# Gate and up of four feed-forward blocks: column tiles in pairs, as seven block products instead of eight

## The chip, the core and the metric

The kernel runs on one core of a Trainium2 chip. The metric is the device time of one execution in microseconds (us). TensorE (PE) multiplies, VectorE (DVE), ScalarE (ACT) and GpSimd (POOL) work on elements, SyncE (SP) issues the transfers.

## What is computed

Two pairs of transformer layers on 512 tokens of width 1024. Each of the four layers ends in a gated feed-forward block, and these four blocks are what the change touches:

```
def swiglu(xn, w_gate, w_up, w_down):
    return (jax.nn.silu(xn @ w_gate) * (xn @ w_up)) @ w_down
```

The hidden width is 2816 = 22 x 128 in all four. Around them stand a mixer of retention, dilated attention and gated MLP (twice), a sparse attention with pooling, a convolution module and two cross attentions, which the change leaves alone.

## The kernel before

All matrix products are made from fp32 numbers split in two fp32r parts, high and low: `mm3` issues three matmuls (high x high, high x low, low x high) for each block of 128 x 128 weights. The activations stand transposed in `xh` and `xl` (8 blocks of 128 features, 512 tokens). The weights come from one stream, `ws`, in the order of use, in tiles of 128 x 1024: `_Weights.prefetch` issues a transfer on SP's queue into one of three `raw` buffers, `_Weights.pump` has ScalarE cast a tile to its high part and VectorE subtract to get the low part, into one of eight `hl` slots. `get` hands out the next tile, `done` gives a slot back.

`ffn` is the block. A column tile of gate or of up (`prod(n, j, ...)`, n the tile, j = 0 gate, 1 up) is 8 blocks x 3 matmuls with the weights stationary and tokens moving, into one PSUM bank. The head of the block makes the tiles n = 0, 1 for tokens 0 to 255, then finishes the norm and the transposes of the last 128-token rows that the stage before left pending (`pend`), then the same tiles for tokens 256 to 511. After that the other 20 tiles of gate and of up run over all 512 tokens. `evac` applies silu on ScalarE into `sg` and multiplies with up on VectorE into `hraw`. The down projection follows, with 22 steps of 24 matmuls; `hsplit` splits a tile of `hraw` in two parts for it.

The order of instructions is written out: a list of `steps` is run by `_Clock`, each step with a length in us that is only used to decide when a transfer counts as arrived and when pending pieces of the norm are due. Each engine runs its instructions in the order in which they are issued, and waits on semaphores.

Of the kernel before, what the change touches and what calls it, by code (L numbers as in the profile page):

```python
# [19 lines left out]
P = 128  # L20
T = 512
# [53 lines left out]
def _weight_tiles(a):  # L75
# [8 lines left out]
    def pairs(w0, w1):  # L84
        for n in range(w0.shape[1] // P):
            yield _rows(w0[:, n * P:(n + 1) * P], 0, KD)
            yield _rows(w1[:, n * P:(n + 1) * P], 0, KD)

    for l in range(DEPTH):
        for name, n in CHUNKS_1:  # L90
            yield from moving(a["w_in"][l][:, COLS_1[name]:COLS_1[name] + n])
        w = a["w_out"][l]
        yield from by_rows(np.concatenate([w[384:768], w[768:1024], w[0:384]]))
        yield from pairs(a["w_gate_up"][l][:, :NF * P], a["w_gate_up"][l][:, NF * P:])
        yield from by_rows(a["w_down"][l])
    for l in range(DEPTH):
# [22 lines left out]
        yield from by_rows(a["cross_wo_2"][l])  # L119
        yield from pairs(a["ffn_w_gate_2"][l], a["ffn_w_up_2"][l])  # L120
        yield from by_rows(a["ffn_w_down_2"][l])
# [70 lines left out]
class _Weights:  # L192
    def __init__(self, nc, raw, hl, src, widths, depth, slots, clock):
# [8 lines left out]
        self.limit = slots  # L202
        self.splits = 0

    def prefetch(self, upto=1 << 30):
        while self.loaded < min(len(self.widths), self.split + self.depth, upto):
            j = self.loaded
            w = abs(self.widths[j])
            self.r[j] = self.raw.tile([P, D], F32, tag="raw", name="raw")
# [4 lines left out]
            self.loaded += 1  # L214

    def pump(self, most=BURST, force=False):
        while most:
# [3 lines left out]
            if self.split < self.loaded and self.splits < self.released + min(self.limit, self.slots):  # L221
# [4 lines left out]
                r = self.r.pop(j)  # L226
                t = self.hl.tile([P, 2, D], F32R, tag="hl", name="hl")
# [4 lines left out]
                self.splits += 1  # L232
                moved = True
            if not moved:
                return

    def get(self):
        j = self.taken
        self.taken += 1
        while j not in self.t and self.widths[j] > 0:  # L240
            self.pump(1, True)
        w = self.widths[j]
        if w < 0:
            self.split += 1
            return self.r.pop(j)[:, :-w], None
        t = self.t.pop(j)
        return t[:, 0, :w], t[:, 1, :w]

    def done(self):
        self.released += 1  # L250


@with_exitstack
def tile_mixers(ctx: ExitStack, tc: tile.TileContext, a: dict, widths: list, out: bass.AP):
# [41 lines left out]
    X = _Clock()  # L296
    W = _Weights(nc, _Bufs(3), _Bufs(8), a["ws"], widths, 3, 8, X)

    def load_x(t):
# [5 lines left out]
    def blocks(b, n=128):  # L305
        return b.rearrange("p (a c) -> p a c", c=n)
# [104 lines left out]
    def g1(key, ts, n, banks, held, evac, fetch=True, free=True, src=None, pump=None):  # L411
# [3 lines left out]
        def step(i):  # L415
            def go():
                if i == 0:
                    st["b"] = [bank(j) for j in banks]
                if fetch:
                    held[key, i] = W.get()  # L420
                wh, wl = (None if w is None else blocks(w, n) for w in held[key, i])
                for kk in range(2):
                    k = 2 * i + kk
                    for b, t in zip(st["b"], ts):
                        if wl is None:
                            PE.matmul(b[:, :n], src[0][:, k, cols(t)], wh[:, kk], start=k == 0, stop=k == KD - 1)
                            continue
                        mm3(b[:, :n], sh[:, k, cols(t)], sl[:, k, cols(t)], wh[:, kk], wl[:, kk], k == 0, k == KD - 1)
                if free:
                    held.pop((key, i))  # L430
                    if wl is not None:
                        W.done()
                if pump is not None:
# [59 lines left out]
    def ffn(pend, post, nxt, last=False):  # L493
# [8 lines left out]
        def evac(n, c0, c1):  # L502
            sg = pl.tile([P, T], F32, tag="sg", name="sg", bufs=2)
            gb, ub = st[n]
            S.activation(sg[:, c0:c1], gb[:, c0:c1], AF.Silu)  # L505
            V.tensor_mul(hraw[:, n, c0:c1], sg[:, c0:c1], ub[:, c0:c1])  # L506

# [24 lines left out]
        steps += [(0.9, p) for p in pend]  # L532
        for n in range(2):
# [7 lines left out]
        hsp = {}  # L541

        def hsplit(k):
            if k < NF:
                hh = pl.tile([P, T], F32R, tag="hh", name="hh", bufs=5)
                hl = pl.tile([P, T], F32R, tag="hlw", name="hlw", bufs=5)
                split_from(hh, hl, hraw[:, k, :])
                hsp[k] = (hh, hl)

# [31 lines left out]

        for i in range(2):
            j = len(steps) - 3 + i
            steps[j] = (steps[j][0], lambda f=steps[j][1], i=i: (f(), hsplit(i)))
        for k in range(NF - TAIL):
# [1166 lines left out]
```

## Time and profile before

| what | value |
|---|---|
| median of 3 runs | 2831.24 us (2827.76 to 2839.96) |
| the profiled execution | 2833.05 us, span of its instructions 2831.3 us |
| mean granted TensorE clock | 0.988 |
| busy share: TensorE, VectorE, ScalarE, GpSimd | 97%, 45%, 36%, 18% |
| transfers | 256 MB, 90 GB/s over the span |

The busy share of an engine is an average over stages with different limits. A matmul's record overlaps the next one's, so a matmul's cost in a stream is the step from start to start.

### The profile page before, as it was taken

Reading aid. Unit: us, or ns where it says so; the run is one execution under the profiler, and the core shown is the slowest. Engines: PE = TensorE matmul, PEld = TensorE weight load, DVE = VectorE, ACT = ScalarE, POOL = GpSimd, SP = SyncE. Lnnn points to the kernel's source line nnn. Section 1 sums busy time; section 2 is a strip of 40 time slices with the busy share of each in tenths; the row PEclk is TensorE's granted clock in tenths of the full one; section 3 lists DMA queues with packets and bytes.
Section 4 is the critical chain, followed back from the end, with each engine's and each line's share of the span. In section 5 each row is a group of like instructions: output and inputs, shape, how many; then the busy total and the mean of one; then the engine's idle time right before and its main releaser. Section 6 shows DMA issues by size and latency. Waiting matters only on the chain.

```text
span 2831.3 us, 34304 instructions
## 1 busy us (share of the span) xinstructions
PE 2739.1 (97%) x13688; PEld 2300.4 (81%) x13688; DVE 1275.2 (45%) x1940; ACT 1018.8 (36%) x1783; POOL 496.7 (18%) x495
## 2 busy tenths in 40 slices
PE   8999999999999999999999999999998889999999
PEld 7888888889788888888677888888886678888887
DVE  4565222344464232454875433233379654432232
ACT  4434222333433222234454433223257445322231
POOL 3231000003131000022461310000049813000000
PEclk9999999999999999999999999999999999999999
DMA  4222322323122223323132213223232212123231
GB/s 156 74 73 75 114 95 97 112 62 109 58 82 85 92 93 108 112 66 107 53 123 82 91 37 119 89 99 124 90 118 90 97 38 90 53 93 101 94 114 52
DMA packets 76192, 255.96 MB, mean 90 GB/s; under 512 B 10368, under 2 KB 11776, under 8 KB 76032
## 3 DMA queue, kind: packets, MB, share of 16 engines
q1 hardware_dynamic: 76032, 253.77, 27.4%
q8 instruction: 107, 1.75, 0.3%
q14 instruction: 53, 0.43, 0.0%
HBM read 251.64 MB, written 2.10 MB: 90 GB/s over the span
## 4 chain that ended last, share of the span: by engine, by line
PE 84%; DVE 8%; ACT 3%; issue 2%; POOL 2%; DMA 0%; ACTq 0%; POOLq 0%; SPq 0%; DVEq 0%
PE b L315 26%; PE b L317 26%; PE b L316 26%; DVE hl L229 1%; DVE b L1527 1%; PE b L337 1%; PE b L1407 1%; PE b L1560 1%; ACT hl L228 1%; DVE mask L1185 1%; PE b L716 1%; POOL sm L322 1%; DVE xn L354 0%; DVE mask L1190 0%; PE b L751 0%
## 5 line engine op out<-in xcount | busy, mean ns | idle before, releaser
L315 PE MATMUL b<-xh,hl 128*128 128x512 f32 (+1 forms) x1728 | 641.2, 371 | 1.6 <-ACT xh L325 1.6
L316 PE MATMUL b<-xl,hl 128*128 128x512 f32 (+1 forms) x1728 | 640.5, 371 | 1.7 <-DVE xl L326 1.7
L317 PE MATMUL b<-xh,hl 128*128 128x512 f32 (+1 forms) x1728 | 639.9, 370 | 0.0
L229 DVE TENSOR_TENSOR hl<-raw,hl 128x1024 fp32r<-128x1024 f32 (+1 forms) x408 | 482.9, 1208 | 152.2 <-ACT hl L228 149.0
L228 ACT CAST hl<-raw 128x1024 fp32r<-128x1024 f32 (+1 forms) x468 | 465.1, 1015 | 114.6 <-PE b L317 76.6
L315 PE MATMUL b<-hl,xh 128*128 128x512 f32 (+2 forms) x1152 | 440.2, 382 | 3.0 <-ACT xh L1630 1.6
L316 PE MATMUL b<-hl,xh 128*128 128x512 f32 (+2 forms) x1152 | 423.6, 368 | 2.0 <-DVE hl L229 2.0
L317 PE MATMUL b<-hl,xl 128*128 128x512 f32 (+2 forms) x1152 | 424.2, 368 | 0.3
L315 PEld LDWEIGHTS b<-xh,hl 128*128 128x128 f32 x1728 | 326.6, 189 | 58.5 <-ACT xh L325 2.8
L316 PEld LDWEIGHTS b<-xl,hl 128*128 128x128 f32 x1728 | 326.5, 189 | 57.6 <-DVE xl L326 2.7
L317 PEld LDWEIGHTS b<-xh,hl 128*128 128x128 f32 x1728 | 326.5, 189 | 55.3
L506 DVE TENSOR_TENSOR hraw<-sg,b 128x512 f32<-128x512 f32 (+1 forms) x96 | 61.8, 643 | 675.3 <-PE b L317 669.7
L505 ACT ACTIVATE sg<-b 128x512 f32<-128x512 f32 (+1 forms) x96 | 54.0, 562 | 673.2 <-PE b L317 673.1
L315 PE MATMUL b<-hl,hh 128*128 128x512 f32 x704 | 274.4, 390 | 0.0
L317 PE MATMUL b<-hl,hlw 128*128 128x512 f32 x704 | 273.9, 389 | 0.0
L316 PE MATMUL b<-hl,hh 128*128 128x512 f32 x704 | 273.9, 389 | 0.0
L315 PEld LDWEIGHTS b<-hl,xh 128*128 128x128 f32 x1152 | 220.1, 191 | 33.2 <-issue 7.0
L316 PEld LDWEIGHTS b<-hl,xh 128*128 128x128 f32 x1152 | 220.2, 191 | 26.1 <-DVE hl L229 3.4
L317 PEld LDWEIGHTS b<-hl,xl 128*128 128x128 f32 x1152 | 219.2, 190 | 26.7 <-DVE xl L326 1.5
L229 POOL TENSOR_TENSOR hl<-raw,hl 128x1024 fp32r<-128x1024 f32 (+2 forms) x60 | 142.3, 2388 | 81.7 <-ACT hl L228 81.5
L326 DVE TENSOR_TENSOR hlw<-hraw,hh 128x512 fp32r<-128x512 f32 x88 | 60.3, 689 | 210.2 <-ACT hh L325 210.2
L317 PEld LDWEIGHTS b<-hl,hlw 128*128 128x128 f32 x704 | 132.2, 188 | 27.4
(272 smaller groups left out, 2974.7 us busy)
## 6 DMA issues: line engine op xcount, KB each, us to landing
raw<-in_ws SPq DMA_DIRECT2D x400, 512.0 KB, 3.5
raw<-in_ws SPq DMA_DIRECT2D x64, 384.0 KB, 3.1
x<-in_x SPq DMA_DIRECT2D x4, 512.0 KB, 6.4
mem<-in_mem SPq DMA_DIRECT2D x4, 512.0 KB, 5.9
out<-x SPq DMA_DIRECT2D x4, 512.0 KB, 2.6
raw<-in_ws SPq DMA_DIRECT2D x4, 336.0 KB, 2.8
gain<-in_g_mix_pre SPq DMA_DIRECT2D x2, 512.0 KB, 5.6
gain<-in_g_mix_post SPq DMA_DIRECT2D x2, 512.0 KB, 4.3
```

What stands on the lines that cost most here:

```text
L228: self.nc.scalar.copy(t[:, 0, :w], r[:, :w])
L229: self.low.tensor_sub(t[:, 1, :w], r[:, :w], t[:, 0, :w].bitcast(F32))
L315: PE.matmul(o, lh, rh, start=first, stop=False)
L316: PE.matmul(o, lh, rl, start=False, stop=False)
L317: PE.matmul(o, ll, rh, start=False, stop=last)
L322: G.tensor_tensor(dst, dst, nhalf[:, :n], op=OP.pow)
L326: (low or V).tensor_sub(dl, src, dh.bitcast(F32))
L337: PE.transpose(b[:, kk * P:(kk + 1) * P], xn[:, k * P:(k + 1) * P], ident)
L505: S.activation(sg[:, c0:c1], gb[:, c0:c1], AF.Silu)
L506: V.tensor_mul(hraw[:, n, c0:c1], sg[:, c0:c1], ub[:, c0:c1])
L716: PE.matmul(s[hh][:, :n], qkT["aq"][rs, pr, cols(t)], qkT["ak"][rs, pr, :n], start=True, stop=True)
L1185: V.scalar_tensor_tensor(mask[t], w[:, :n], iw[:, t, h:h + 1], acc, op0=OP.mult, op1=OP.add)
```

## The change

The tiles n = 0, 1 and the head stay. The other 20 tiles of gate and 20 of up are taken two by two: a unit is a pair of column tiles (n, n + 1) of gate or of up, 256 columns x 1024 features of weights, over 512 tokens. The activations are cut in four blocks (features 0 to 511 or 512 to 1023, tokens 0 to 255 or 256 to 511) and the weights in four (features, column tile), and the unit's result is made of seven products of such blocks or of sums of them, each 4 blocks x 3 matmuls of 256 tokens, into banks 0 to 4 and half of bank 5 or 6 each (`todo` in `seven`). Two units, gate and up, make a pair of hidden tiles; there are 20 units in each block.

The sums of activations are made once for each block in the head, full sums in unused parts of `hraw` (`whole`, `mix`), then high and low parts (`sum_high`, `sum_low`) in new `sh` tiles or in `xh`, `xl`. The sums of weights are made for each unit (`_Weights.unit`): `t13` two differences of 512 columns on GpSimd, `t24` two on VectorE, in place in the raw tiles, then four slots are cast and subtracted (`cast1`, `low1` to `cast3`, `low3`; slot 4 has 512 columns). The preparation of unit i + 1 is issued between the products of unit i. The sums of results are a copy on ScalarE (`m1`) and six VectorE instructions in `s2`, `s4`, `s5`, `s6` and `whole_sum`. silu runs in place on a pair of tiles, and `gated` multiplies a pair. The second raw tile of a unit goes to the two `xn` buffers. The gains of the next stage (`nxt`) are loaded after gate and up instead of in the head.

```diff
+    def seven(w0, w1):
+        yield from pairs(w0[:, :2 * P], w1[:, :2 * P])
+        for n in range(2, w0.shape[1] // P, 2):
+            for w in (w0, w1):
+                for c in (n, n + 1):
+                    yield _rows(w[:, c * P:(c + 1) * P], 0, KD), True
...
+        def t13():
+            b = u["b"] = self.r.pop(u["j"])
+            u["b12"], u["b22"] = (b[:, 512 * i:512 * i + 512] for i in range(2))
+            G.tensor_sub(u["b11"], u["b12"], u["b11"])
+            G.tensor_sub(u["b12"], u["b12"], u["b22"])
+
+        def t24():
+            V.tensor_sub(u["b22"], u["b22"], u["b11"])
+            V.tensor_sub(u["b21"], u["b21"], u["b22"])
...
-        for n in range(2, NF):
-            for j in range(2):
-                steps.append(prod(n, j, 0, 512, True, True))
-        steps[8] = (steps[8][0], lambda f=steps[8][1]: (nxt(), f()))
...
+        def product(i, x, w, o):
+            (xa, xb), (wa, wb) = act[x], unit(i)["w" + w]()
+            for k in range(4):
+                mm3(o, wa[:, k], wb[:, k], xa[:, k], xb[:, k], k == 0, k == 3)
...
+            def whole_sum():
+                V.tensor_add(c[:, :, 256:], u3[:, None, :].to_broadcast([P, 2, 256]), halves(b45))
+                if not j:
+                    S.activation(c, c, AF.Silu)
+
+            def gated():
+                if j:
+                    V.tensor_mul(hraw[:, n:n + 2, :], hraw[:, n:n + 2, :], c)
+            done.append((whole_sum, gated))
+            last = done[-2] if i else (lambda: None,) * 2
+
+            def s0():
+                last[0]()
+                W.done(int(i > 0))
+                prep(i + 1, "low1")
+
+            def s1():
+                S.copy(m1, p1)
+                prep(i + 1, "t13")
+                last[1]()
+
+            def s2():
+                V.tensor_add(c[:, 0, TOK[0]], m1, p2)
+                prep(i + 1, "cast4")
+                W.done()
+
+            def s3():
+                prep(i + 1, "low4")
+                W.done()
+
+            def s4():
+                V.tensor_add(u2, m1, p6)
+                prep(i + 1, "t24", "cast2")
+
+            def s5():
+                V.tensor_add(u3, u2, p7)
+                prep(i + 1, "low2", "cast3")
+                W.done()
+
+            def s6():
+                V.tensor_add(u4, u2, p5)
+                V.tensor_add(c[:, 1, TOK[0]], u4, p3)
+                prep(i + 1, "low3")
+                prep(i + 2, "cast1")
+            todo = (("a11", "b11", p1), ("a12", "b21", p2), ("s4", "b22", p3), ("s2", "t2", p6), ("s3", "t3", p7), ("s1", "t1", p5),
+                    ("a22", "t4", p4))
...
+        also(0, whole(1, 0, 0, G), unit0("cast1"))
+        also(1, whole(2, 4, 0, G), unit0("low1"))
+        also(late, whole(0, 0, 1, G), whole(3, 4, 1, V), mix(3, 0, 3, 1), mix(0, 0, 1, 0))
+        also(late + 1, unit0("t13", "cast4", "low4", "t24", "cast2"), sum_high("s3", 0), mix(1, 3, 1, 0), mix(2, 2, 1, 0))
+        also(late + 2, unit0("low2", "cast3"), sum_high("s2", 1), sum_low("s3", 0), sum_high("s4", 2))
+        also(late + 3, scratch, unit0("low3"), lambda: prep(1, "cast1"), sum_low("s2", 1), sum_low("s4", 2), sum_high("s1", 3), sum_low("s1", 3))
```

VectorE's queue in the first gate-and-up stage, before, where two hidden tiles are made (L506 is the product with up, L229 a weight tile's low part, `raw` the tile as it came, `hl` its slot):

```order
L506 TENSOR_TENSOR hraw_2338<-sg_2668,b5_2619 128x512
L229 TENSOR_TENSOR hl_2671<-raw_2524,hl_2671 128x1024
L229 TENSOR_TENSOR hl_2676<-raw_2556,hl_2676 128x1024
L229 TENSOR_TENSOR hl_2707<-raw_2585,hl_2707 128x1024
L506 TENSOR_TENSOR hraw_2338<-sg_2736,b7_2682 128x512
```

The same queue in the changed kernel, for one unit that has a gate product (L675 the late sum, L270 low parts, L681 the gate product, L287 and L288 the sums of `t24`, the others sums of results; `b` are PSUM banks, `pc` scratch in SBUF):

```order
L675 TENSOR_TENSOR hraw_2336<-pc_2624,b6_2755 128x2x256
L270 TENSOR_TENSOR hl_2866<-raw_2626,hl_2866 128x1024
L681 TENSOR_TENSOR hraw_2336<-hraw_2336 128x1024
L696 TENSOR_TENSOR hraw_2336<-pc_2624,b1_2869 128x256
L270 TENSOR_TENSOR hl_2917<-raw_2727,hl_2917 128x512
L705 TENSOR_TENSOR pc_2624<-pc_2624,b3_2871 128x256
L287 TENSOR_TENSOR raw_2727<-raw_2727,raw_2626 128x512
L288 TENSOR_TENSOR raw_2626<-raw_2626,raw_2727 128x512
L709 TENSOR_TENSOR pc_2624<-pc_2624,b4_2872 128x256
L270 TENSOR_TENSOR hl_2947<-raw_2727,hl_2947 128x1024
L714 TENSOR_TENSOR pc_2624<-pc_2624,b5_2873 128x256
L715 TENSOR_TENSOR hraw_2336<-pc_2624,b2_2870 128x256
```

One L270 of 1024 columns follows and ends the unit. Five instructions for two hidden tiles (four column tiles) have become 12 or 13 for one pair of column tiles. L287 waits for GpSimd, the L270 behind L709 for ScalarE's cast.

GpSimd's queue from the last norm's root (L391, L392) on, in the changed kernel; before, nothing follows there until the stage's end:

```order
L391 TENSOR_SCALAR sm_2415<-sm_2414 128x1
L392 TENSOR_TENSOR sm_2415<-sm_2415,nhalf_64 128x1
L620 TENSOR_TENSOR hraw_2336<-xh_66,xl_67 128x1024
L283 TENSOR_TENSOR raw_2275<-raw_2486,raw_2275 128x512
L284 TENSOR_TENSOR raw_2486<-raw_2486 128x512
L283 TENSOR_TENSOR raw_2488<-raw_2490,raw_2488 128x512
L284 TENSOR_TENSOR raw_2490<-raw_2490 128x512
```

Two more L620 stand ahead of L391. L620 are full sums of activations, L283 and L284 the differences of `t13`, two for each unit.

VectorE's queue in the second half of the head, changed kernel, behind one full sum (L620) and two mixes (L624), as far as the low part of the sum that the third product takes (L571 is `evac`'s product, L635 low parts of the activations' sums):

```order
L571 TENSOR_TENSOR hraw_2336<-hraw_2336,b1_2352 128x256
L270 TENSOR_TENSOR hl_2550<-raw_2486,hl_2550 128x512
L287 TENSOR_TENSOR raw_2486<-raw_2486,raw_2275 128x512
L288 TENSOR_TENSOR raw_2275<-raw_2275,raw_2486 128x512
L624 TENSOR_TENSOR hraw_2336<-hraw_2336 128x1024 x2
L270 TENSOR_TENSOR hl_2555<-raw_2486,hl_2555 128x1024
L635 TENSOR_TENSOR sh_2558<-hraw_2336,sh_2557 128x1024
L571 TENSOR_TENSOR hraw_2336<-hraw_2336,b3_2420 128x256
L270 TENSOR_TENSOR hl_2589<-raw_2275,hl_2589 128x1024
L635 TENSOR_TENSOR sh_2592<-hraw_2336,sh_2591 128x1024
L635 TENSOR_TENSOR sh_2596<-hraw_2336,sh_2595 128x1024
```

Before, this stretch of the queue holds the two products of `evac` and three low parts of weights.

## Rows read from the trace of the kernel before

**Rows 1.** The page's first lines: the span, and of each engine busy us, share of the span and count of instructions.

```profile
span 2831.3 us, 34304 instructions
PE 2739.1 (97%) x13688; PEld 2300.4 (81%) x13688; DVE 1275.2 (45%) x1940; ACT 1018.8 (36%) x1783; POOL 496.7 (18%) x495
```

**Rows 2.** The table of stretches, over the 512-column parts of the four gate-and-up stages: the stretch, its length, busy us (and instructions) of PE, PEld, DVE, ACT and POOL, granted clock, share of the transfer engines, GB/s.

```profile
294.00:512.00 218.00, 218.00 (x964) 180.58 (x963) 59.08 (x62) 54.95 (x67) 0.00 (x0) 1.00 0.30 101
916.00:1134.00 218.00, 218.00 (x964) 180.52 (x964) 59.00 (x62) 54.85 (x67) 0.00 (x0) 1.00 0.31 100
1731.00:1949.00 218.00, 218.00 (x966) 180.63 (x966) 58.96 (x61) 54.44 (x67) 0.00 (x0) 1.00 0.29 99
2489.00:2707.00 218.00, 218.00 (x967) 180.66 (x965) 58.96 (x61) 54.71 (x67) 0.00 (x0) 1.00 0.29 96
```

**Rows 3.** TensorE in order of time (start, length, what, shape): the first and the last of the 960 matmuls of 512 columns in the first stage, and the first of the down projection.

```profile
293.98 0.40 PE L315 MATMUL b<-xh,hl 128*128 128x512 f32 x1
...
511.38 0.39 PE L317 MATMUL b<-xh,hl 128*128 128x512 f32 x1
511.60 0.39 PE L315 MATMUL b<-hl,hh 128*128 128x512 f32 x1
```

**Rows 4.** TensorE in order of time: the first and the last of 94 matmuls of 256 columns that follow each other in the head of the first stage.

```profile
282.70 0.28 PE L317 MATMUL b<-xh,hl 128*128 128x256 f32 x1
...
293.86 0.29 PE L317 MATMUL b<-xh,hl 128*128 128x256 f32 x1
```

**Rows 5.** VectorE in order of time, three places in the first stage and its head; in square brackets idle time ahead and who ended it. L385 waits for the result of L381, L229 behind it for nothing of VectorE's.

```profile
261.74 1.40 DVE L381 SCALAR_TENSOR_TENSOR xn<-b,sm,gain 128x512 f32<-128x512 f32 x2
263.18 1.22 DVE L385 TENSOR_TENSOR x<-x,xn 128x1024 f32<-128x1024 f32 x1
264.32 1.22 DVE L229 TENSOR_TENSOR hl<-raw,hl 128x1024 fp32r<-128x1024 f32 x1
...
274.93 0.42 DVE L506 TENSOR_TENSOR hraw<-sg,b 128x256 f32<-128x256 f32 x1 [0.34 <-PE b L317]
275.27 2.35 DVE L229 TENSOR_TENSOR hl<-raw,hl 128x1024 fp32r<-128x1024 f32 x2
...
305.15 0.69 DVE L506 TENSOR_TENSOR hraw<-sg,b 128x512 f32<-128x512 f32 x1 [10.48 <-PE b L317]
305.76 3.49 DVE L229 TENSOR_TENSOR hl<-raw,hl 128x1024 fp32r<-128x1024 f32 x3
```

**Rows 6.** VectorE and ScalarE in order of time: a VectorE instruction and the ScalarE one that waits for it, a ScalarE cast and the VectorE instruction that waits for it, and the group of all casts of 1024 columns (count, busy us, mean ns of one, idle time ahead).

```profile
273.36 1.23 DVE L385 TENSOR_TENSOR x<-x,xn 128x1024 f32<-128x1024 f32 x1
274.68 1.06 ACT L349 ACTIVATE xn<-x 128x1024 f32<-128x1024 f32 x1 [0.36 <-DVE x L385]
...
282.07 1.06 ACT L228 CAST hl<-raw 128x1024 fp32r<-128x1024 f32 x1
283.17 1.23 DVE L229 TENSOR_TENSOR hl<-raw,hl 128x1024 fp32r<-128x1024 f32 x1
...
L228 ACT CAST hl<-raw 128x1024 fp32r<-128x1024 f32 x400 | 409.6, 1047 | 91.5 <-PE b L317 60.3 <-DMA raw<-in_ws 25.4 <-issue 4.4
```

**Rows 7.** GpSimd and VectorE at the same time, in order of time at two places; GpSimd where VectorE doesn't hold it; and groups of the stretch 2130 to 2200 us (count, busy us, mean ns), in which GpSimd never stops. L1519 and L229 read two SBUF tensors, L1527 one and a PSUM bank.

```profile
636.45 7.40 POOL L229 TENSOR_TENSOR hl<-raw,hl 128x768 fp32r<-128x768 f32 x3
636.52 2.85 DVE L354 SCALAR_TENSOR_TENSOR xn<-x,sm,gain 128x1024 f32<-128x1024 f32 x1 [1.53 <-POOL sm L322]
...
2201.45 5.64 DVE L229 TENSOR_TENSOR hl<-raw,hl 128x1024 fp32r<-128x1024 f32 x3 [0.62 <-ACT hl L228]
2201.78 4.24 POOL L1519 TENSOR_TENSOR y<-y,m 128x512 f32<-128x512 f32 x2
...
2225.83 1.29 POOL L1519 TENSOR_TENSOR y<-y,m 128x512 f32<-128x512 f32 x1
2227.07 2.37 POOL L229 TENSOR_TENSOR hl<-raw,hl 128x1024 fp32r<-128x1024 f32 x1
...
L1519 POOL TENSOR_TENSOR y<-y,m 128x512 f32<-128x512 f32 x38 | 60.9, 1602 | 4.7 <-ACT m L1518 1.8
L1527 DVE SCALAR_TENSOR_TENSOR b<-hp,conv_w,b 128x512 f32<-128x512 f32 x64 | 43.5, 741 | 0.0
L229 DVE TENSOR_TENSOR hl<-raw,hl 128x1024 fp32r<-128x1024 f32 x12 | 18.2, 1522 | 0.0
```

**Rows 8.** The head of the first stage in order of time, where the pending norm ends: GpSimd's root, VectorE's scaling, TensorE's transposes, the last low parts of the activations, and the first matmul on them.

```profile
276.66 1.38 POOL L322 TENSOR_TENSOR sm<-sm,nhalf 128x1 f32<-128x1 f32 x1
278.07 1.28 DVE L354 SCALAR_TENSOR_TENSOR xn<-x,sm,gain 128x1024 f32<-128x1024 f32 x1 [0.45 <-POOL sm L322]
280.43 1.03 PE L337 MATMUL b<-ident,xn 128*128 128x128 f32 x8
281.73 1.29 DVE L326 TENSOR_TENSOR xl<-b,xh 128x512 fp32r<-128x512 f32 x2 [0.62 <-ACT xh L325]
282.48 0.39 PE L316 MATMUL b<-xl,hl 128*128 128x256 f32 x1 [0.34 <-DVE xl L326]
```

More of the change, by code (lines that the diff above doesn't have):

```diff
@@ L203, in __init__ @@
         self.splits = 0
+        self.held, self.odd, self.raw2, self.two = [0, 0], False, None, 0
     def prefetch(self, upto=1 << 30):
-        while self.loaded < min(len(self.widths), self.split + self.depth, upto):
+        while self.loaded < min(len(self.widths), upto):
             j = self.loaded
             w = abs(self.widths[j])
-            self.r[j] = self.raw.tile([P, D], F32, tag="raw", name="raw")
+            second = self.widths[j] < 0 and self.odd
+            if self.held[second] == (self.depth, self.two)[second]:
+                return
+            self.odd = self.widths[j] < 0 and not self.odd
+            self.held[second] += 1
+            pl, tag = (self.raw, "raw") if not second else (self.raw2, "xn")
+            self.r[j] = pl.tile([P, D], F32, tag=tag, name="raw")
             o = int(self.offs[j])
@@ L214, in prefetch, with slot @@
             self.loaded += 1
+    def slot(self):
+        assert self.splits < self.released + self.slots
+        self.splits += 1
+        return self.hl.tile([P, 2, D], F32R, tag="hl", name="hl")
     def pump(self, most=BURST, force=False):
@@ L226, in pump @@
                 r = self.r.pop(j)
-                t = self.hl.tile([P, 2, D], F32R, tag="hl", name="hl")
+                self.held[0] -= 1
+                t = self.slot()
                 self.nc.scalar.copy(t[:, 0, :w], r[:, :w])
@@ L235, in pump, with unit, cast, go @@
                 return
+    def unit(self):
+        V, S, G = self.nc.vector, self.nc.scalar, self.nc.gpsimd
+        u = {}
+        def cast(name, src, n=D):
+            def go():
+                if name not in u:
+                    u[name] = self.slot()
+                S.copy(u[name][:, 0, :n], src())
+            return go
+        def low(name, src, n=D):
+            return lambda: V.tensor_sub(u[name][:, 1, :n], src(), u[name][:, 0, :n].bitcast(F32))
+        def fetch():
+            while self.widths[self.split] > 0:
+                self.pump(1, True)
+            self.prefetch()
+            u["a"], u["j"] = self.r.pop(self.split), self.split + 1
+            self.split += 2
+            u["b11"], u["b21"] = (u["a"][:, 512 * i:512 * i + 512] for i in range(2))
+        def t13():
[6 more added lines that the diff above has]
+            V.tensor_sub(u["b21"], u["b21"], u["b22"])
+        def free(i):
+            def go():
+                self.held[i] -= 1
+                self.prefetch()
+            return go
+        one, two, last = (lambda: u["a"]), (lambda: u["b"]), (lambda: u["b22"])
+        u["do"] = {
+            "cast1": (fetch, cast("s1", one)), "low1": (low("s1", one),), "t13": (t13,), "t24": (t24,),
+            "cast2": (cast("s2", two),), "low2": (low("s2", two), free(1)), "cast4": (cast("s4", last, 512),),
+            "low4": (low("s4", last, 512),), "cast3": (cast("s3", one),), "low3": (low("s3", one), free(0)),
+        }
+        for k, slot, i in (("b11", "s1", 0), ("b21", "s1", 1), ("t3", "s2", 0), ("t2", "s2", 1), ("b22", "s4", 0),
+                           ("t1", "s3", 0), ("t4", "s3", 1)):
+            u["w" + k] = lambda slot=slot, i=i: [
+                u[slot][:, z, 512 * i:512 * i + 512].rearrange("p (a c) -> p a c", c=P) for z in range(2)]
+        return u
@@ L532, in ffn @@
         steps += [(0.9, p) for p in pend]
+        steps.append((0, lambda: two(2)))
         for n in range(2):
@@ new lines, in sum_low, with unit, prep @@
+        def sum_low(k, i):
+            return lambda: V.tensor_sub(act[k][1], quarter(full(i)), act[k][0].bitcast(F32))
+        units = [(n, j) for n in range(2, NF, 2) for j in range(2)]
+        ops, done, hsp = {}, [], {}
+        def unit(i):
+            if i not in ops:
+                ops[i] = W.unit()
+            return ops[i]
+        def prep(i, *names):
+            if 0 <= i < len(units):
+                for name in names:
+                    for f in unit(i)["do"][name]:
+                        f()
@@ new lines, in scratch, with also, unit0 @@
+        def scratch():
+            st["pc"] = base.tile([P, D], F32, tag="g0", name="pc")
+        def hsplit(k):
+            if k < NF and k not in hsp:
+                t = shared()
+                split_from(t[:, 0:T], t[:, T:2 * T], hraw[:, k, :])
+                hsp[k] = (t[:, 0:T], t[:, T:2 * T])
+        def also(i, *fs):
+            us, g = steps[i]
+            steps[i] = (us, lambda: (g(), [f() for f in fs]))
+        late = len(steps) - 4
+        def unit0(*names):
+            return lambda: prep(0, *names)
@@ L550, in ffn, with last_sums @@
+        def last_sums():
+            done[-1][0]()
+            W.done()
+            done[-1][1]()
+        for i in range(len(units)):
+            g = seven(i)
+            steps += [(12 * 0.119, lambda g=g: next(g))] * 7
+        steps.append((0, last_sums))
+        steps.append((0, lambda: (two(0), nxt(), hsplit(1))))
         TAIL = 4
```

88 lines of the change are left out of this document (60 added, 28 removed).

## The prediction

> **What bounds the kernel now.** I read the page's busy shares first, then the table of stretches over the four gate-and-up stages, then single instructions in time order. TensorE is busy 97% of the span [rows 1], and in the four stages it is busy without a gap, 218.00 of 218.00 us each, at a granted clock of 1.00; VectorE is busy 59 us of the 218 there, ScalarE 55, GpSimd not at all [rows 2]. So in these stages only TensorE's work counts, and the others have room that the change means to use. One stage's 512-column part runs from 293.98 to 511.60, where the down projection starts, with 960 matmuls (40 column tiles of 24): 226.7 ns each [rows 3]. The 256-column form that the change uses everywhere stands in the head of each stage: from 282.70 to 293.86 there are 94, hence 93 steps: 120.0 ns each [rows 4]. Half of 226.7 would be 113.3; the short form pays 6.7 ns more.
>
> **What is removed from TensorE.** A unit is two column tiles of gate or of up. Before: 2 x 24 matmuls of 512 columns = 48 x 0.2267 = 10.88 us. After: seven products of 4 x 3 matmuls of 256 columns = 84 x 0.1200 = 10.08 us. Gain 0.80 us a unit; ten pairs of column tiles, gate and up, four stages are 80 units: **64.1 us**. The eighth that is saved in arithmetic (1.36 us) is cut by the dearer short form. The Trainium skill, "TensorE: Matmul & The Clock Gate", section on the back-to-back issue gap, gives a gap of N/2.4 + 2.5 ns, 109.2 ns for 256 columns and 215.8 for 512. By it the gain would be 48 x 0.2158 - 84 x 0.1092 = 1.19 us a unit, 95 us in all; both rows are 11 ns longer than it says, and I go by the rows. The operands are those of the head (weights stationary, 256 columns of activations moving), so I see no reason for another step.
>
> **What is added on VectorE, one unit.** VectorE runs its queue in order. Its step from one instruction to the next is shorter than the record: two 1024-column differences take 2.35 us with one record at 1.22, so a step is 1.13; 512 columns step 0.61 (305.15 to 305.76), 256 columns with one input in PSUM 0.34 (274.93 to 275.27) [rows 5]. An instruction that waits for its own engine's result starts 0.04 us behind that record's end (263.14 to 263.18), not 0.08 ahead of it, as 264.32 against 264.40: 0.11 to 0.12 us more [rows 5]. In order of the queue, a unit has: the late sum of the unit before (512 columns, 0.61), a low part (1.13), in every second unit the gate product (1.13), a 256-column sum (0.34), the low part of the fourth slot (0.61), another sum (0.34), two 512-column weight sums of which the second needs the first (0.72 + 0.61), a sum (0.34), a low part (1.13), two sums, the second on the first (0.45 + 0.34), a low part (1.13). Work: 7.75 us, 8.88 with the gate product.
>
> Two waits come on top. First, the low part behind the weight sums needs ScalarE's cast of the first sum: 0.69 (its record) + 0.09 to ScalarE (274.59 to 274.68) + 1.05 for the cast + 0.04 back (283.13 to 283.17) = 1.83 [rows 5, 6], while VectorE has 0.72 + 0.61 + 0.34 = 1.67 to do: 0.16 idle. Second, GpSimd. It makes two 512-column weight differences a unit, 1.27 us each (1.29 in the record, 1.24 to the next) [rows 7]. Where both engines read two SBUF tensors they exclude each other: a 1024-column VectorE instruction that takes 1.28 took 2.85 beside GpSimd's, and three differences beside two GpSimd sums took 5.64 instead of 3.49, 1.07 more for each of the two [rows 5, 7, 8]. It is one for one: who waits gets in when the other ends. Instructions with one input in PSUM are not held: 64 of them took 741 ns in the stretch where GpSimd never stops, while the 1024-column differences there went from 1.22 to 1.52 [rows 7].
>
> So, from the end of the first low part's step: GpSimd starts at 0.13 and holds the ports to 1.20; the 256-column sum runs beside it; the fourth slot's low part runs 1.20 to 1.81; GpSimd's second runs 1.81 to 3.08 with a sum beside it; the weight sums, which need it, start at 3.12. VectorE has worked 1.29 of that. With the gate product in front (GpSimd then starts at 1.13) it is 4.12. A unit is thus 0.61 + 1.13 + 3.12 + 1.67 + 0.16 + 1.13 + 0.45 + 0.34 + 1.13 = **9.74 us**, and **10.74** with the gate product: a pair 20.48, against TensorE's 20.16. VectorE just fails to keep up, by 0.32 a pair. The Trainium skill, "VectorE: DVE Perf Modes", section on the DRAIN, says that a semaphore between chained instructions costs nothing. By it a pair would be 0.44 shorter, 20.04, and VectorE would keep up; rows 5 show the 0.11, and I keep it.
>
> VectorE may lag: weights are made five products (7 us) ahead. What is tight is the bank of the third product. Its sum is the last but one instruction of a unit and ends 1.0 us before the unit does; TensorE wants the bank 2.88 us (two products) into the next unit. So the lag at a unit's start may be 13.96 less the unit's length: 4.2, and 3.2 where a gate product comes. ScalarE's share (3.7 us of casts, a copy, every second unit a silu that I price as the 1.06 us squaring [rows 6]) hides behind that, DMA too (as many tiles as before, at 100 GB/s).
>
> **What is added at the head.** Four sums of activations must exist before the third product of the first unit. Before, the last low part of the activations ends at 281.73 + 1.29 = 283.02 and TensorE leaves the head at 293.98, 10.96 later [rows 3, 8]. Counting from 283.02, VectorE with GpSimd's three instructions between: full sum to 1.16; GpSimd's full sum (2.37, [rows 7]) to 3.53; its first weight difference to 4.80; mix 4.60 to 5.73; second difference to 7.00; mix 6.80 to 7.93; product 8.27; low part 8.88; weight sums 9.60, 10.21; two mixes 11.34, 12.59; low part, sum's low part 13.72, 14.85; product 15.19; low part 16.32; low parts of the second and fourth-slot sums 17.45, 18.58. TensorE comes to the third product at 10.96 + 2.88 = 13.84 and starts at 18.7: **4.9 us**, four times 19.6. The bounds are 2 (no exclusion: GpSimd's four blocks of about 1 us go) and 8 (each self-wait and handover 0.2 worse).
>
> Further ahead, GpSimd's two early full sums stand before the last norm's root. In the first two stages the 1024-column residual add (273.36) falls between them and ends some 2.9 later; the scaled rows, ready at 279.35 before with the transposes at 280.43, come at 281.2: 0.8 us, twice [rows 6, 8]. The other two stages have no such add: nothing.
>
> After the stall the first unit's lag works out to 2.9, so two pairs pass free and seven pay 0.32: 2.2 us a stage, 9 in all (bounds 0 and, at 0.6 more a pair, 29). The end of the stage costs nothing: the last unit has no weight preparation, and the first down weights and hidden tile are split in it.
>
> **Sum.** The profiled execution took 2833.05 (span 2831.3), 1.8 above the median of the runs. 2833 - 64.1 + 19.6 + 1.6 + 9 = 2799; **2798** as a median.
>
> **Rivals.** (B) VectorE keeps up and the head stall is near its lower bound: 2833 - 64 + 12 = 2781. For it: one step 0.16 us a unit shorter suffices. (C) GpSimd keeps the ports for both differences in a row: 0.3 more a unit, pair 21.1, 0.9 late a pair, some 7 us a stage: 2819. Against it: rows 7 show turns. (D) Slower: GpSimd's differences take 1.7 here, each blocking VectorE 0.43 longer. A pair grows by 1.7 to 22.2, 2.0 over TensorE's, 18 us a stage, and the gain is gone: 2833 - 64 + 21 + 73 = 2863. It decides from a pair of about 21.4. For it: the mean in the contended stretch is 1.60; against it: that holds the waiting, which I count apart. (E) The short matmuls step slower when fed by new tiles: from 0.129 there is no gain, 2850.
>
> **How the numbers follow.** A (the sum, own range 2785 to 2815) 0.48, B 0.22, C 0.14, D 0.13, E 0.03. About 0.5% (14 us) is what a measurement can tell. Faster: most of A, B, a third of C: 0.74; slower: D and part of E: 0.14; the rest 0.12. The range 2776 to 2838 holds A, B and C and most of their bounds.
>
> **What would show it.** In the changed profile: 256-column steps of 0.120 in the stages; VectorE busy over 80% there; GpSimd's two differences stretched beyond 1.27; TensorE waiting some 5 us for a VectorE low part at the third product of each stage, then a few tenths in later units, for VectorE. Units of 10.1 to 10.3 on average bear A out; 10.08 flat is B; over 10.7 is D, and makes the prediction wrong. So would a lowered clock behind the head's stall: rows 2 show 1.00, but no such stall is in them.

## The result, and the profile after

The changed kernel takes 2804.86 us (median of 4 runs, 2802.16 to 2806.56) where the kernel before takes 2834.33 (4 runs, 2827.76 to 2839.96): ratio 0.9896, 95% interval 0.9870 to 0.9922, so it is faster by 1.0%. The profiled execution took 2806.56, 26.5 less than the one before.

The page of the changed kernel, first lines and three groups (they answer to [rows 1]):

```profile
span 2804.8 us, 41537 instructions
PE 2678.5 (96%) x16568; PEld 2383.2 (85%) x16568; DVE 1830.9 (65%) x2737; ACT 1172.7 (42%) x1999; POOL 793.5 (28%) x666
...
L283 POOL TENSOR_TENSOR raw<-raw 128x512 f32<-128x512 f32 x80 | 140.5, 1757 | 552.1 <-DVE hl L270 552.1
L386 PE MATMUL b<-sh,hl 128*128 128x256 f32 x960 | 272.6, 284 | 14.4 <-DVE sh L635 14.4
L385 PE MATMUL b<-sh,hl 128*128 128x256 f32 x960 | 275.0, 286 | 7.7 <-DVE hraw L715 6.2
```

TensorE now waits in two places that did not exist: 14.4 us for VectorE's low part of an activation sum (`sh`, L635), and 6.2 for a sum of results (L715). GpSimd's difference takes 1757 ns on average where the operation takes 1.27 us by itself.

The row of the table of stretches for the seven-product part (it answers to [rows 2], same columns), the first stage; in the others VectorE is busy 176.61 us of 203, 176.57 of 202 and 175.62 of 202:

```profile
303.00:505.00 202.00, 200.06 (x1648) 198.96 (x1649) 175.68 (x242) 83.50 (x108) 63.67 (x38) 0.99 0.29 96
```

VectorE went from 59 busy us of 218 to 176 of 202, and TensorE has gaps. From its first to its last gate-and-up matmul, a stage took 242.5 us before; now the four take 235.01, 235.02, 234.17 and 234.91. The sum went from 970.1 to 939.1: 31.0 less. The rest of the program is 4.5 longer.

**The head's wait.** TensorE at the third product of the first unit, and where its steps are short again:

```profile
298.72 0.28 PE L387 MATMUL b<-xh,hl 128*128 128x256 f32 x1
299.38 0.38 PE L385 MATMUL b<-sh,hl 128*128 128x256 f32 x1 [0.39 <-ACT hraw L570]
303.36 0.58 PE L386 MATMUL b<-sh,hl 128*128 128x256 f32 x1 [3.60 <-DVE sh L635]
303.74 0.41 PE L387 MATMUL b<-sh,hl 128*128 128x256 f32 x1
...
308.43 0.31 PE L385 MATMUL b<-sh,hl 128*128 128x256 f32 x1
308.58 0.28 PE L386 MATMUL b<-sh,hl 128*128 128x256 f32 x1
...
309.40 0.28 PE L387 MATMUL b<-sh,hl 128*128 128x256 f32 x1
```

Starts 0.66 and 3.98 apart instead of 0.12 are 4.4 us lost. Then comes something that the sum had no term for: 22 steps of 0.213 us up to 308.43. The stretches of the same execution show why; the granted clock is the number behind GpSimd's column:

```profile
300.00:303.00 3.00, 0.00 (x0) 0.00 (x0) 3.00 (x3) 2.00 (x4) 0.00 (x0) 0.77 0.61 223
303.50:308.40 4.90, 4.90 (x23) 4.90 (x24) 4.03 (x4) 0.00 (x0) 2.61 (x2) 0.50 0.04 16
309.00:330.00 21.00, 21.00 (x179) 21.00 (x178) 18.32 (x26) 8.62 (x11) 6.08 (x4) 1.00 0.32 101
```

While TensorE waited, its clock fell from 2.4 to 1.2 GHz and stayed there for 4.9 us of full work: 23 matmuls where 41 would fit at 0.119 us each. With the slow first step that is 2.3 us a stage (1.6 in the third, where the slow steps are fewer).

**The later waits.** VectorE through one unit without a gate product, and GpSimd's two differences beside it:

```profile
397.12 0.68 DVE L675 TENSOR_TENSOR hraw<-pc,b 128x512 f32<-128x512 f32 x1
397.72 1.22 DVE L270 TENSOR_TENSOR hl<-raw,hl 128x1024 fp32r<-128x1024 f32 x1
399.18 0.42 DVE L696 TENSOR_TENSOR hraw<-pc,b 128x256 f32<-128x256 f32 x1 [0.25 <-ACT pc L691]
399.70 1.15 DVE L270 TENSOR_TENSOR hl<-raw,hl 128x512 fp32r<-128x512 f32 x1
400.78 0.41 DVE L705 TENSOR_TENSOR pc<-pc,b 128x256 f32<-128x256 f32 x1
402.05 0.69 DVE L287 TENSOR_TENSOR raw<-raw 128x512 f32<-128x512 f32 x1 [0.86 <-POOL raw L284]
402.77 0.69 DVE L288 TENSOR_TENSOR raw<-raw 128x512 f32<-128x512 f32 x1
...
399.01 1.30 POOL L283 TENSOR_TENSOR raw<-raw 128x512 f32<-128x512 f32 x1 [6.79 <-DVE hl L270]
400.39 1.62 POOL L284 TENSOR_TENSOR raw<-raw 128x512 f32<-128x512 f32 x1
```

The low part of 512 columns (399.70) lasts 1.15 instead of 0.68, since GpSimd holds the ports until 400.3; GpSimd's second record (400.39) begins while VectorE still has them and ends at 402.01, and only then L287 can start. The late sums (L675) of the first stage follow each other by 9.80 and 10.70 us in turn: 20.50 a pair, TensorE's pair being 20.01. For some seven units after the head nothing shows of it, then it does, once a pair:

```profile
395.68 0.28 PE L387 MATMUL b<-xh,hl 128*128 128x256 f32 x1
396.21 0.36 PE L385 MATMUL b<-sh,hl 128*128 128x256 f32 x1 [0.25 <-DVE hraw L715]
396.41 0.28 PE L386 MATMUL b<-sh,hl 128*128 128x256 f32 x1
```

Six such waits cost 3.1 us a stage (0.41 each for the wait, and 0.08 for the next step).

### The profile page after: what moved, and what is told of

It is laid out like the page before. It is cut to its first block, busy times and chain, and to the rows that moved or that the text cites. A ratio compares the mean times of both kernels' runs of the same rounds, so it can differ in the third digit from the quotient of the medians.

```text
span 2804.8 us, 41537 instructions
## 1 busy us (share of the span) xinstructions
PE 2678.5 (96%) x16568; PEld 2383.2 (85%) x16568; DVE 1830.9 (65%) x2737; ACT 1172.7 (42%) x1999; POOL 793.5 (28%) x666
## 4 chain that ended last, share of the span: by engine, by line
PE 55%; DVE 19%; ACT 10%; POOL 10%; issue 4%; DMA 1%; POOLq 0%; SPq 0%; DVEq 0%; ACTq 0%
PE b L385 16%; PE b L387 16%; PE b L386 16%; ACT hl L266 6%; DVE hl L270 5%; POOL raw L283 4%; POOL raw L284 4%; DVE raw L287 2%; DVE hl L250 2%; DVE hraw L675 1%; DVE b L1736 1%; ACT hl L249 1%; PE b L407 1%; PE b L1616 1%; DVE xn L424 1%
## 5 line engine op out<-in xcount | busy, mean ns | idle before, releaser
L385 PE MATMUL b<-xh,hl 128*128 128x256 f32 (+1 forms) x1728 | 504.7, 292 | 1.6 <-ACT xh L395 1.6
L386 PE MATMUL b<-xl,hl 128*128 128x256 f32 (+1 forms) x1728 | 503.7, 291 | 1.7 <-DVE xl L396 1.7
L387 PE MATMUL b<-xh,hl 128*128 128x256 f32 (+1 forms) x1728 | 503.3, 291 | 0.0
L266 ACT CAST hl<-raw 128x1024 fp32r<-128x1024 f32 x320 | 286.5, 940 | 411.6 <-DVE raw L287 411.6
L385 PE MATMUL b<-hl,xh 128*128 128x512 f32 (+2 forms) x1152 | 439.5, 381 | 4.9 <-ACT xh L395 3.1
L270 DVE TENSOR_TENSOR hl<-raw,hl 128x1024 fp32r<-128x1024 f32 x320 | 387.9, 1212 | 8.1
L250 DVE TENSOR_TENSOR hl<-raw,hl 128x1024 fp32r<-128x1024 f32 (+2 forms) x249 | 304.2, 1236 | 132.9 <-ACT hl L249 130.7
L249 ACT CAST hl<-raw 128x1024 fp32r<-128x1024 f32 (+2 forms) x308 | 303.6, 1001 | 101.4 <-PE b L387 56.7
L385 PEld LDWEIGHTS b<-xh,hl 128*128 128x128 f32 x1728 | 331.2, 192 | 8.3 <-ACT xh L395 2.8
L387 PEld LDWEIGHTS b<-xh,hl 128*128 128x128 f32 x1728 | 330.9, 192 | 5.2
L283 POOL TENSOR_TENSOR raw<-raw 128x512 f32<-128x512 f32 x80 | 140.5, 1757 | 552.1 <-DVE hl L270 552.1
L386 PE MATMUL b<-sh,hl 128*128 128x256 f32 x960 | 272.6, 284 | 14.4 <-DVE sh L635 14.4
L385 PE MATMUL b<-sh,hl 128*128 128x256 f32 x960 | 275.0, 286 | 7.7 <-DVE hraw L715 6.2
L387 PE MATMUL b<-hl,sh 128*128 128x512 f32 x704 | 274.4, 390 | 0.4
L385 PE MATMUL b<-hl,sh 128*128 128x512 f32 x704 | 274.5, 390 | 0.0
L386 PE MATMUL b<-hl,sh 128*128 128x512 f32 x704 | 274.0, 389 | 0.0
L387 PE MATMUL b<-sh,hl 128*128 128x256 f32 x960 | 271.8, 283 | 0.0
L385 PEld LDWEIGHTS b<-hl,xh 128*128 128x128 f32 x1152 | 219.4, 190 | 34.9 <-issue 7.0
```

Of the source, the lines that this page charges most:

```text
L266: S.copy(u[name][:, 0, :n], src())
L270: return lambda: V.tensor_sub(u[name][:, 1, :n], src(), u[name][:, 0, :n].bitcast(F32))
L283: G.tensor_sub(u["b11"], u["b12"], u["b11"])
L385: PE.matmul(o, lh, rh, start=first, stop=False)
L386: PE.matmul(o, lh, rl, start=False, stop=False)
L387: PE.matmul(o, ll, rh, start=False, stop=last)
```

## The experiments

The table shows by how much the steps of TensorE are longer than 0.119 us, from the first matmul on `sh` to the stage's end, in us a stage, mean of the four. The last column is the sum of the four stages' lengths. The 0.3 of two kernels is slow first steps behind a wait, at the full clock. "Again" is the changed kernel a second time, beside the fill. The parts and the lengths of stages agree to 0.4 us a stage.

| kernel | head's wait | half clock and first step | wait in the second unit | later waits | four stages |
|---|---|---|---|---|---|
| changed | 4.4 | 2.2 | 0 | 3.1 | 939.1 |
| again | 4.4 | 2.3 | 0 | 3.1 | 939.8 |
| differences on VectorE | 3.8 | 2.5 | 0 | 0 | 925.8 |
| new head | 0.9 | 0.3 | 1.9 | 4.7 | 930.6 |
| both | 0.9 | 0.3 | 1.4 | 0 | 910.5 |
| filled wait | 1.5 + 2.9 of fill | 0.1 | 0 | 4.4 | 934.2 |

**The differences on VectorE.** My theory was that GpSimd's work costs VectorE more than it spares it; the rival, that VectorE has too much work whoever does the differences.

```diff
-            G.tensor_sub(u["b11"], u["b12"], u["b11"])
-            G.tensor_sub(u["b12"], u["b12"], u["b22"])
+            V.tensor_sub(u["b11"], u["b12"], u["b11"])
+            V.tensor_sub(u["b12"], u["b12"], u["b22"])
```

> GpSimd's two weight differences of each unit are made by VectorE instead. My theory (VectorE idles 1.8 us a unit because GpSimd holds the shared ports and the first weight sum waits for it): VectorE's queue gets 1.22 us of work more and loses the 1.83 us of waiting, so a pair of units falls from 20.5 to about 19.5 us, under TensorE's 20.0; the six stalls of 0.4 us in each stage go, 10 us in all, and the head's stall shrinks by about 1 us four times. Time about 2791. Rival (VectorE's amount of work is what makes it lag, the waiting lies beside other waits): a pair grows by 2.4 to 22.9 us and the time by about 95 us, to 2900.

Measured: 2790.75 us (ratio 0.9838, 0.9824 to 0.9853). The stretch of the first stage, and TensorE at the third product:

```profile
303.00:500.00 197.00, 197.00 (x1644) 197.00 (x1644) 187.56 (x281) 85.72 (x110) 0.00 (x0) 0.99 0.29 100
```

```profile
300.83 0.58 PE L386 MATMUL b<-sh,hl 128*128 128x256 f32 x1 [3.59 <-DVE sh L635]
```

VectorE does more, 187.56 of 197 us, and TensorE never waits for it: the later waits are gone in all four stages. The late sums follow each other by 9.34 and 10.68, a pair 20.02, TensorE's pace. That is longer than I expected (19.5), and VectorE waits for other engines only twice between 310 and 490 us of the span, 1.6 us in all, so it has next to nothing left over. What was the matter was the sharing, not the work: VectorE does two instructions more in each unit and its pair is still 0.48 shorter. The head's wait falls by only 0.6, and the half clock behind it stays.

**A new order in the head.** All late sums and the first unit's differences on VectorE, the sums that the third product needs ahead of the rest; GpSimd keeps the later units.

```diff
-        also(late, whole(0, 0, 1, G), whole(3, 4, 1, V), mix(3, 0, 3, 1), mix(0, 0, 1, 0))
-        also(late + 1, unit0("t13", "cast4", "low4", "t24", "cast2"), sum_high("s3", 0), mix(1, 3, 1, 0), mix(2, 2, 1, 0))
-        also(late + 2, unit0("low2", "cast3"), sum_high("s2", 1), sum_low("s3", 0), sum_high("s4", 2))
...
+        also(late, whole(0, 0, 1, V), whole(3, 4, 1, V), mix(3, 0, 3, 1), mix(0, 0, 1, 0), mix(1, 3, 1, 0), mix(2, 2, 1, 0))
+        also(late + 1, unit0("t13", "cast4", "low4"), sum_high("s4", 2), sum_high("s2", 1), sum_low("s4", 2), unit0("t24", "cast2"), sum_high("s3", 0))
+        also(late + 2, unit0("cast3", "low2"), sum_low("s2", 1), sum_low("s3", 0))
```

> Head alone: all sums behind the last transposes, and the first unit's weight differences, are made by VectorE, in the order in which the products want them (the third product's sum first); the units after the first keep GpSimd's differences. My theory: the third product's stall (4.4 us) goes, and with it the half clock of some 3 to 5 us behind it (2 us more), four times. But VectorE then starts the units about 6 us behind, over the limit of 4.2 and 3.2, so about 2 us come back at the second unit and the 0.5 us a pair is paid from the first pair on: about 2 to 3 us a stage gained, time about 2796. Rival (the lag at the start does not matter, only the stall): 6.6 us a stage, 2779.

Measured: 2798.74 us (0.9862, 0.9846 to 0.9879), by the whole time not told apart from the changed kernel; its four stages are 930.6, 8.5 shorter. The head's wait falls to 0.9 and no half clock follows. But TensorE is then early, and the lag shows sooner; its wait in the second unit, and the granted clock behind that:

```profile
311.46 0.36 PE L386 MATMUL b<-sh,hl 128*128 128x256 f32 x1 [1.62 <-DVE hraw L717]
...
311.60:316.00 4.40, 4.40 (x38) 4.40 (x39) 4.05 (x5) 1.84 (x3) 1.66 (x2) 1.00 0.64 232
```

The head gives back 5.4 us a stage, 3.5 of the wait and 1.9 of the clock. Of these, 1.9 are lost again in the second unit, and 1.6 by nine later waits instead of six. While VectorE is slower than TensorE, a wait that is taken away at the front partly comes back behind.

**Both.** The two edits together, GpSimd's differences on VectorE everywhere.

> Both: all weight differences by VectorE and the new order in the head. My theory: no stall at the third product, full clock, about 1 us at the second unit, and none later since a pair takes VectorE about 19.5 us: 8 us a stage, time about 2772. If the two gains are not independent (the lag of the head is never made up), about 2785. If VectorE's amount of work is the limit: over 2880.

Measured: **2770.03 us** (2769.31 to 2773.63; 0.9768, 0.9753 to 0.9783), the fastest kernel here. The two waits that the first stage has left behind the head's transposes:

```profile
297.99 0.39 PE L385 MATMUL b<-sh,hl 128*128 128x256 f32 x1 [0.64 <-ACT hraw L570]
...
309.62 0.35 PE L385 MATMUL b<-sh,hl 128*128 128x256 f32 x1 [1.20 <-DVE hraw L715]
```

The stages are 28.6 us shorter than the changed kernel's, where the two edits alone give 13.3 and 8.5: the head's gain is kept once VectorE keeps up. The whole gained more than the stages. Its profiled execution is 37.3 us shorter than the changed kernel's, and 8.7 of these lie outside the four stages (5.7 against the second profile of the changed kernel), in code that the edits leave alone. So it is partly luck that the time came out so near the 2772 expected: the stages gave 7.2 us each instead of 8.

Most of the 8.7 lie in the two stretches from the first stage to the second and from the second to the third, which are 2.9 and 5.2 shorter. TensorE has the same matmuls there; its busy time is 2.8 and 3.1 us less, at a granted clock of 1.00 against 0.99. Why the clock fell less there is open.

**A filled wait.** To separate the half clock from the head's wait: the first product is made twice more into a bank that nobody reads, ahead of the third product.

```diff
+                if i == 0 and r == 2:
+                    spare = bank(7)
+                    for _ in range(2):
+                        product(0, "a11", "b11", spare[:, :256])
```

> The changed kernel, with the first product of the first unit made twice more into an unused bank ahead of the third product, so that TensorE works through 2.9 of the 4.4 us in which it waits there. My theory: the wait costs what it did, but the half clock behind it does not come, and the 2.1 us a stage go that the first 24 matmuls lose there (1.4 in the third stage): about 8 us, 2797. Rival (the lower clock comes from the whole stage's load, not from the wait): no gain, 2805.

TensorE at the third product, and the granted clock around it:

```profile
299.58 0.28 PE L385 MATMUL b<-sh,hl 128*128 128x256 f32 x1
301.20 0.39 PE L386 MATMUL b<-sh,hl 128*128 128x256 f32 x1 [1.34 <-DVE sh L635]
```

```profile
301.00:304.00 3.00, 2.79 (x23) 2.80 (x24) 3.00 (x5) 0.00 (x0) 0.44 (x1) 1.00 0.19 70
304.00:310.00 6.00, 6.00 (x53) 6.00 (x52) 5.02 (x8) 2.69 (x3) 2.48 (x2) 1.00 0.00 0
```

The third product starts no earlier (2.9 + 1.5 is 4.4 again), and the clock stays at 1.00. The load of the stage is otherwise as it was, so it was the idle time that took the clock down. Of the 2.2 us a stage, later waits take 1.2 to 1.3 back, eight of them instead of six; the stages are 4.9 to 5.6 shorter instead of the 8 expected. The whole is 2802.73 (0.9891, 0.9877 to 0.9906), which is not told apart from the changed kernel's 2798.11 beside it.

> The changed kernel as it is, beside the others on the same chip: 2805, ratio 0.9896 within 0.002.

Measured: 2798.11 (2796.95 to 2804.38; 0.9873, 0.9857 to 0.9890), a ratio 0.0023 under the first set's, a little over the 0.002 expected; the two intervals overlap.

**The short form alone.** The kernel before with each column tile as two halves of 256 tokens: the same work, twice the matmuls.

```diff
-                steps.append(prod(n, j, 0, 512, True, True))
+                steps.append(prod(n, j, 0, 512, True, True, 2))
```

> The kernel before, with each column tile behind the head made in two halves of 256 tokens (twice as many matmuls of half the width; nothing else is changed): the price of the short form by itself. My theory: 96 steps of 0.119 to 0.120 us instead of 48 of 0.2267 for two column tiles, 0.55 to 0.64 us more for each of 80 units: 44 to 51 us slower, about 2882. Rival (the dearer step of the head is a thing of the head): no slower.

```profile
294.00:525.00 231.00, 231.00 (x1928) 231.00 (x1927) 58.97 (x61) 53.80 (x66) 0.00 (x0) 1.00 0.28 98
```

TensorE has no gap, 1928 matmuls in 231 us are 0.120 each, and the stages are 51.5 longer (2884.52 in one run). The dearer form costs what the prediction took from [rows 4].

**The weights of the next stage.** In the changed kernel VectorE makes three low parts for the mixer behind the down projection (L250, at 619.27, 622.72 and 624.79) among the down projection's last norms. In the kernel before GpSimd makes three, behind the norms (636.45 in [rows 7]). The first and the last of VectorE's three:

```profile
619.27 0.95 DVE L250 TENSOR_TENSOR hl<-raw,hl 128x768 fp32r<-128x768 f32 x1
...
624.79 0.95 DVE L250 TENSOR_TENSOR hl<-raw,hl 128x768 fp32r<-128x768 f32 x1
```

The first two down projections are 1.9 us longer than before (third 1.2, fourth 0.4). I let the planner take transfers as arrived earlier from there on.

```diff
-        steps.append((0, lambda: (two(0), nxt(), hsplit(1))))
+        steps.append((0, lambda: (two(0), setattr(W, "lead", 4.0), nxt(), hsplit(1))))
```

> As the changed kernel, but from the down projection on a weight tile counts as arrived 4 us after its issue instead of 9 in the planner's clock. My theory: the three low parts of the next stage's weights that stand among the last norms of the down projection move ahead of them, and the 1.2 to 1.9 us that TensorE waits there in three of four stages go: about 5 us. Rival (TensorE waits there for something else): no change in the down projection's length (123.7, 123.7, 122.4, 119.8 us).

One run: 2805.72, so the 5 us did not come. The down projections get 1.5, 1.5, 0.6 and 0 us shorter, and the mixer behind the first takes 257.6 instead of 255.5. The changed kernel and the one before differ in the same way, and here are their rows, in this order; the first stretch is the first down projection, the second the mixer behind it:

```profile
505.90:629.60 123.70, 122.01 (x545) 100.42 (x544) 55.41 (x64) 41.47 (x64) 5.70 (x10) 1.00 0.33 108
629.60:885.10 255.50, 242.65 (x1437) 214.28 (x1436) 139.56 (x260) 100.68 (x201) 64.57 (x72) 0.99 0.23 74
```

```profile
511.60:633.40 121.80, 121.74 (x545) 100.49 (x544) 50.44 (x56) 36.74 (x58) 4.18 (x10) 1.00 0.28 88
633.40:890.90 257.50, 243.87 (x1438) 215.37 (x1437) 135.98 (x259) 100.79 (x201) 68.31 (x73) 0.98 0.24 76
```

Together they take 379.2 and 379.3 us. With the low parts among the norms the down projection is 1.9 longer and the mixer 2.0 shorter. But of the 2.0 in the mixer 1.2 are TensorE's own busy time, at a granted clock of 0.98 before and 0.99 in the changed kernel, so not all of it is moved work.

**Both, with that edit.**

> All together: weight differences by VectorE, the new order in the head, and the earlier arrival of weights in the down projection. My theory: 2770 less up to 4 us, 2767.

Measured: 2777.39 (2775.10 to 2778.65; 0.9801, 0.9786 to 0.9815), worse than without it. Its stages are the same (910.4), the first two down projections 1.5 shorter, but what follows them is longer by 4.9 and 5.4. The traces show where: over the whole stretches from the first stage to the second and from the second to the third, which are 3.3 and 3.9 us longer, TensorE is busy 366.0 and 553.3 us instead of 361.9 and 547.7, with as many matmuls, at a granted clock of 0.99 instead of 1.00. So it is TensorE's clock that fell more, not a wait that grew. What brought it down is open: the two kernels ran on different chips (the kernel before took 2835.88 and 2833.42 beside them), and two profiles of the changed kernel differ by up to 2.3 us in such stretches, in both directions.

## Why the prediction was right

The median was to be 2798 and is 2804.86 in one set of runs and 2798.11 in the other; both are inside the own range of case A, the likeliest. The sum from 2833.05 gave -34, the profiled execution shows -26.5. The mechanisms that the prediction named are the ones that the traces show: a gain on TensorE, a wait at the third product and a drift of VectorE. That the total came so near is in part luck, because terms that were wrong offset each other. Term by term, for all four stages:

- **The gain on TensorE**: 64.1 forecast, 70 measured. The step on the `sh` operands is 0.118 at the full clock (308.58 to 309.40 are seven), on `xh` 0.120 as in [rows 4]; 84 steps take 10.00 us instead of 10.08. That the operands make a difference was not in the rows of before.
- **The head's wait**: 19.6 forecast, 17.6 measured (4.4 a stage). Counted from the last low part of the activations (285.01 in the first stage), TensorE reached the product at 13.83 and the sum's low part came at 18.3; forecast were 13.84 and 18.58. These are VectorE's rows at the two ends of that count, the last low part of the activations and the sum's low part (the second of the two in the row, which ends at 303.31):

```profile
283.72 1.29 DVE L396 TENSOR_TENSOR xl<-b,xh 128x512 fp32r<-128x512 f32 x2 [0.62 <-ACT xh L395]
...
300.96 2.35 DVE L635 TENSOR_TENSOR sh<-hraw,sh 128x1024 fp32r<-128x1024 f32 x2
```

- **The clock behind it**: 0 forecast, 8.6 measured. The prediction named a lowered clock behind the head's stall among the signs that would make it wrong, and did not price it, because no row of the kernel before has such a stall in these stages. The sign came, and the total held only because other terms were off the other way. The filled wait shows it to be the idle time's consequence.
- **VectorE's unit**: 9.74 and 10.74 forecast, 9.80 and 10.70 measured, a pair 20.48 and 20.50. From the end of the first low part's step L287 was to start at 3.12; in the rows above it is 402.05 - 398.85 = 3.20. The exclusion one for one, the self-wait (L287 to L288 step 0.72, L288 to the next 0.61) and the sums from PSUM that run free beside GpSimd all hold.
- **The drift**: 9 forecast, 12.4 measured, because TensorE's pair is 20.01 and not 20.16: VectorE fails by 0.49 a pair, not 0.32, in six pairs a stage.
- **The early full sums ahead of the norm's root**: 1.6 forecast, 0 measured. This step failed. It had the residual add end some 2.9 later and the scaled rows 1.85 later (281.2 instead of 279.35). The add ends only 1.6 later against the head's start, one low part of the weights no longer stands ahead of the scaling, and the scaled rows come only 0.4 later (281.73 - 270.81 = 10.92, before 279.35 - 268.83 = 10.52), inside the 1.08 by which they were early [rows 8]:

```profile
276.21 2.00 DVE L455 TENSOR_TENSOR x<-x,xn 128x1024 f32<-128x1024 f32 x1
...
278.46 1.21 DVE L270 TENSOR_TENSOR hl<-raw,hl 128x1024 fp32r<-128x1024 f32 x1
280.45 1.28 DVE L424 SCALAR_TENSOR_TENSOR xn<-x,sm,gain 128x1024 f32<-128x1024 f32 x1 [0.77 <-POOL sm L392]
```

- **The end of the stage at nothing**: right on balance at the first stage, where down projection and mixer together are as long as before. I had not looked past the stage at what the same stream of weights does to the next one.
- **Outside**: 4.5 us more that no term has. 2.0 of them lie ahead of the first stage (268.83 and 270.81), in code that the change leaves alone; the second profile of the changed kernel reaches that stage at 267.62. The rest lies mostly between the second and third stage, 575.2 against 573.1. The second profile has 573.1 there too, but 2.3 more than the first between the third stage and the fourth. So these parts vary from one execution to the next by as much as the term is large.

So -70 + 17.6 + 8.6 + 12.4 + 4.5 = -27, against the -26.5 seen. The forecast came out near because a gain too small by 6, a stall too dear by 2 and a cost of 1.6 that never came stood against a clock not priced (8.6), a drift too small by 3.4 and the 4.5 outside: 9.5 one way and 16.5 the other.

Of the rivals, B (VectorE keeps up, 2781) needed what the experiment with the differences on VectorE did; C (GpSimd keeps the ports for both) falls with the order of the rows at 399.01 to 402.05, where VectorE's low part runs between. D took GpSimd's difference at 1.7: its records do last 1757 and 1649 ns on average, but they contain the wait for the ports (a first one in a free stretch, 399.01, takes 1.30), as the prediction held. E fell with the step of 0.118 to 0.120.

## What to carry to other kernels

Fewer multiplications on TensorE are worth what the engine that prepares them can keep up with: write out one whole period of that engine's queue, with the port sharing and the waits on its own results, and compare it with TensorE's period, since a shortfall of 2% becomes a wait in every period. Before giving work to GpSimd beside a full VectorE, count it as VectorE's too: here two differences of 1.27 us taken over by GpSimd cost VectorE more than doing them itself at 0.6 to 0.7. When a comparison is about a few us, look at the granted clock outside the changed stages as well: 8.7 of the best kernel's 37.3 us lie there. When a stall is removed at the front of a stage, see first whether the stage behind can use the time; here the head's edit gave 8.5 us alone and 15.3 once the differences were on VectorE.

## What the runs showed of the hardware

- A wait of TensorE of 3.6 us, after full work, brought the granted clock down to 0.50, and TensorE worked at that for 4.9 us (303.50 to 308.40) before it was 1.00 again; waits of 1.34 us (filled wait) and 1.62 us (new head) left it at 1.00. The head's wait cost 4.4 us in all, and the clock 2.3 more.
- VectorE and GpSimd, both on SBUF alone, take turns instruction by instruction: a VectorE instruction of 0.68 lasted 1.15 behind GpSimd's 1.30, and GpSimd's 1.27 showed as 1.62 behind VectorE. The Trainium skill, "SBUF — State Buffer", section "SBUF: two separate sides", says that the engines share one pair of ports as an exclusive lock which an instruction keeps to its end, and the other fully blocks. The traces agree with these numbers.
- An instruction on VectorE that needs the result of the one ahead starts 0.11 later than one that does not (0.72 against 0.61 at 402.05 to 403.38, in every unit). The Trainium skill, "VectorE: DVE Perf Modes", section on the DRAIN, says that a semaphore between chained instructions costs nothing extra; the measurement decides. With two such places in a unit it is, by the prediction's sum, 0.44 of the 0.49 us by which VectorE's pair is longer than TensorE's; no run took it away by itself.
- A matmul of 256 columns steps by 0.118 us on the `sh` tiles and by 0.120 on `xh` and `xl`, in the same shape and with weights from the same kind of tile (`hl`). Why was not tried.
- The kernel with both edits is also some 4 to 10 us shorter outside the four stages than the other kernels, in code that its edits don't touch. The mean granted clock of its execution is 0.992 (0.983 to 0.989 in the others), and in the two stretches where it gains most TensorE is busy less for the same matmuls. So TensorE's clock accounts for most of it; what held the clock up is open.
